# Hybrid decoder layer on one core: the last layer norm's mean taken out of the weights and the residual, its squares on ScalarE

## Chip, core and metric

The kernel runs on one core of a Trainium2 chip. The metric is the device time of one execution in microseconds (us). Engines are called PE (TensorE), DVE (VectorE), ACT (ScalarE), POOL (GpSimd) and SP (SyncE, which here issues every DMA).

## What is computed

One post-norm decoder layer over 256 tokens of width 1024. The input is normalized, projected to 3844 columns, and sent through four mixers (SSD, HGRN2, retention, block attention), each of which gives 256 columns of y. The four are put side by side, multiplied with an output weight, added to the scaled input and normalized again:

```python
def _layernorm(x, g, b):
    xf = x.astype(F32)
    mu = jnp.mean(xf, -1, keepdims=True)
    var = jnp.mean(jnp.square(xf - mu), -1, keepdims=True)
    return ((xf - mu) * lax.rsqrt(var + LN_EPS) * g + b).astype(x.dtype)
...
    y_cat = jnp.concatenate([y_ssd, y_hgrn, y_ret, y_moba], axis=-1).astype(x.dtype)
    y = jnp.einsum('blm,md->bld', y_cat, w_out)
    return _layernorm(DEEPNORM_ALPHA * x + y, ln_g, ln_b)
```

## The kernel before

Everything is in SBUF at once: the 256 tokens are two blocks T = 0, 1 of 128 partitions. Each matmul of float32 data is made of three passes on parts: every operand is split in a high part (rounded, type fp32r) and a low part (the rest), and hi x hi, hi x lo and lo x hi are summed in PSUM. For weights this split is `split_hi` (L215, a copy on ACT, L222) and `split_lo` (L224, a subtraction on DVE, L231). For the mixers' outputs it is `y_split` (L420: ACT at L422, DVE at L423).

The order of the work is written by hand. There are 38 weight tiles of 512 KB: 15 column units of the input projection with two halves each (tiles 0 to 29), then the output weight as four pairs of row blocks (`ORDER`, 256 rows each) with two column halves of 512 each (tiles 30 to 37, shape 128 x 2 x 512, `wr_wo`). The program runs in slots. `begin(slot)` (L1046) issues the load of tile slot + 6 (`load_w`, five raw buffers), splits tile slot + 4 on ACT, runs the mixers' steps that a table `steps` (L1007) lists for this slot, and then makes the low part of tile slot + 4 on DVE. After that come the matmuls of the slot's own tile (`project`). So ACT and DVE take their work in the order in which it is written here, and work of a step stands in the same queue as the weights' splits.

From slot 30 on the matmuls are those of the output projection (`oproj`, L969), in the order of the list at L1064: blocks i = 0, 1, 2 of T = 0 (each 12 matmuls over 512 columns), block 0 of T = 1, block 3 of T = 0, and then the rest of T = 1 by column pieces (512, 256, 256; `OCOLS`). `begin` of slots 30 to 37 stands between them, and four transposes of the retention's y before block 2. The names in the profile are `po` for the sums in PSUM, `whi_wo` and `wlo_wo` for the weight's parts.

The residual (`residual`, L961, one for each T, in slots 21 and 22) makes alpha * x of the first norm's output from rows that a DMA broadcast to all partitions (`load_rows`, tile `rb`). The last norm's rows are loaded into the same buffer right behind, so this second load waits for the second residual. After the last matmul of a column piece `out_add` (L984) adds the residual and takes statistics; after the last piece `out_norm` (L989) joins these, makes the inverse root on POOL (`rsqrt_of`, L251), and applies norm, weight and bias on DVE, with a store per piece.

Of the kernel before, what the change touches and what calls it, by code (L numbers as in the profile page):

```python
# [119 lines left out]
def hybrid_layer(  # L120
# [21 lines left out]
    def sb(shape, name, tag=None, dt=F32, bufs=1):  # L142
        return sp.tile(shape, dt, name=name, tag=tag or name, bufs=bufs)
# [24 lines left out]
    mhalf = cp.tile([P, 8], F32, name="mhalf")  # L168
    nc.gpsimd.memset(mhalf, -0.5)


# [783 lines left out]
    def load_rows(first):  # L955
# [3 lines left out]
        rowt[first] = t  # L959

    def residual(T):  # L961
        rb = rowt[0]
        nc.vector.scalar_tensor_tensor(xn[T], xn[T], ALPHA, rb[:, 0, :], op0=ALU.mult, op1=ALU.mult)
        nc.vector.scalar_tensor_tensor(xn[T], rb[:, 1, :], ALPHA, xn[T], op0=ALU.mult, op1=ALU.add)

# [15 lines left out]

    fst = [sb([P, len(OCOLS[T]) - 1, 6], f"fst{T}") for T in range(NT)]

    def out_add(T, n):  # L984
        cs = slice(OCOLS[T][n], OCOLS[T][n + 1])
        nc.vector.tensor_add(xn[T][:, cs], xn[T][:, cs], po[T, cs.start])  # L986
        nc.vector.bn_stats(fst[T][:, n, :], xn[T][:, cs])

    def out_norm(T):  # L989
        rb = rowt[2]  # L990
        m_ = sb([P, 2], f"fmv{T}")
        nc.vector.bn_aggr(m_, fst[T])
        rs = sb([P, 1], f"frs{T}")
        rsqrt_of(rs, m_[:, 1:2], 1.0, LN_EPS)
        cuts = [slice(a, b) for a, b in zip(OCOLS[T], OCOLS[T][1:])]
        for cs in (slice(0, 512), slice(512, 1024)):
            nc.vector.scalar_tensor_tensor(xn[T][:, cs], xn[T][:, cs], m_[:, 0:1], rb[:, 0, cs],
                                           op0=ALU.subtract, op1=ALU.mult)
        for cs in cuts:
            nc.vector.scalar_tensor_tensor(xn[T][:, cs], xn[T][:, cs], rs[:, 0:1], rb[:, 1, cs],  # L1000
                                           op0=ALU.mult, op1=ALU.add)
            nc.sync.dma_start(out[T * P:(T + 1) * P, cs], xn[T][:, cs])
# [43 lines left out]
    def begin(slot):  # L1046
        if slot < 32:
            load_w(*divmod(slot + 6, 2))
        if slot < 34:
            split_hi(*divmod(slot + 4, 2))  # L1050
        for st in steps.get(slot, []):
            st()
        if slot < 34:
            split_lo(*divmod(slot + 4, 2))

    first_unit()
# [62 lines left out]
```

## Time and profile before

| | before |
|---|---|
| median of 3 runs | 150.22 us (150.21 to 150.48) |
| the profiled execution | 150.22 us, its span 148.5 us |
| PE busy | 136.9 us, 92% of the span |
| DVE busy | 116.4 us, 78% |
| ACT busy | 74.7 us, 50% |
| POOL busy | 17.8 us, 12% |
| mean granted PE clock | 0.977 |

The span runs from the first to the last recorded instruction; the 1.7 us between it and the execution's time lie around it. Busy time is not yet a bound: PE is the engine on the chain that ended last for nearly the whole span, and the others matter where it waits for them.

### The profile page before, as it was taken

Reading aid. Unit: us, or ns where it says so; the run is one execution under the profiler, and the core shown is the slowest. Engines: PE = TensorE matmul, PEld = TensorE weight load, DVE = VectorE, ACT = ScalarE, POOL = GpSimd, SP = SyncE. Lnnn points to the kernel's source line nnn. Section 1 sums busy time; section 2 is a strip of 40 time slices with the busy share of each in tenths; the row PEclk is TensorE's granted clock in tenths of the full one; section 3 lists DMA queues with packets and bytes.
Section 4 is the critical chain, followed back from the end, with each engine's and each line's share of the span. In section 5 each row is a group of like instructions: output and inputs, shape, how many; then the busy total and the mean of one; then the engine's idle time right before and its main releaser. Section 6 shows DMA issues by size and latency. Waiting matters only on the chain.

```text
span 148.5 us, 3256 instructions
## 1 busy us (share of the span) xinstructions
PE 136.9 (92%) x1320; PEld 127.0 (86%) x1320; DVE 116.4 (78%) x240; ACT 74.7 (50%) x120; POOL 17.8 (12%) x23
## 2 busy tenths in 40 slices
PE   5679999999999999999999999999999999999800
PEld 3169999999999998999999999999999988888800
DVE  1789978989495498969897699976889898078681
ACT  3089969643360859699909950053861953000000
POOL 4230000000000000000062018014004000004040
PEclk9968999999999999999999999999999999999995
DMA  4998399989758340647615820279765440000304
GB/s 155 288 385 342 87 321 339 306 302 348 224 151 224 127 109 32 173 182 248 178 75 145 309 118 0 55 238 385 234 228 141 141 141 4 0 0 0 141 0 141
DMA packets 9390, 26.07 MB, mean 176 GB/s; under 512 B 1056, under 2 KB 1696, under 8 KB 9120
## 3 DMA queue, kind: packets, MB, share of 16 engines
q1 hardware_dynamic: 9376, 25.87, 52.9%
q8 instruction: 10, 0.16, 0.5%
q14 instruction: 4, 0.03, 0.1%
HBM read 24.82 MB, written 1.05 MB: 174 GB/s over the span
## 4 chain that ended last, share of the span: by engine, by line
PE 89%; DMA 3%; DVE 3%; SPq 1%; POOLq 1%; POOL 1%; issue 0%; DVEq 0%
PE po L979 5%; PE po L980 5%; PE po L978 5%; PE pj_h_f L343 4%; PE pj_z L406 4%; PE pj_xs L406 4%; PE pj_m_v L406 4%; PE pj_m_k L406 4%; PE pj_h_g L406 4%; PE pj_m_g L406 4%; PE pj_m_q L406 4%; PE pj_bc L406 4%; PE pj_r_k L406 4%; PE pj_r_g L406 4%; PE pj_h_i L406 4%; PE pj_r_v L406 4%
## 5 line engine op out<-in xcount | busy, mean ns | idle before, releaser
L979 PE MATMUL po<-wlo_wo,yhi 128*128 128x512 f32 (+1 forms) x40 | 14.0, 350 | 0.0
L978 PE MATMUL po<-whi_wo,yhi 128*128 128x512 f32 (+1 forms) x40 | 14.0, 349 | 0.0
L980 PE MATMUL po<-whi_wo,ylo 128*128 128x512 f32 (+1 forms) x40 | 13.9, 347 | 0.0
L222 ACT CAST whi_wo<-wr_wo 128x1024 fp32r<-128x1024 f32 x8 | 8.3, 1051 | 3.3 <-DMA wr_wo<-in_wo_dram 1.9
L231 DVE TENSOR_TENSOR wlo_wo<-wr_wo,whi_wo 128x1024 fp32r<-128x1024 f32 x8 | 9.6, 1218 | 0.0
L693 POOL TENSOR_SCALAR_AFFINE_SELECT ra<-ahi 128x1024 fp32r<-128x1024 f32 x1 | 1.1, 1102 | 65.1 <-DVE ahi L689 65.1
L978 PEld LDWEIGHTS po<-whi_wo,yhi 128*128 128x128 f32 x40 | 7.5, 188 | 1.0
L980 PEld LDWEIGHTS po<-whi_wo,ylo 128*128 128x128 f32 x40 | 7.5, 188 | 1.0
L979 PEld LDWEIGHTS po<-wlo_wo,yhi 128*128 128x128 f32 x40 | 7.5, 188 | 1.0
L986 DVE TENSOR_TENSOR xn<-xn,po 128x512 f32<-128x512 f32 (+1 forms) x5 | 2.9, 579 | 5.8 <-PE po L980 5.8
L637 DVE SCALAR_TENSOR_TENSOR cacc_xs<-pj_xs,ch,cacc_xs 128x255 f32<-128x255 f32 (+2 forms) x6 | 2.9, 482 | 4.6 <-ACT cacc_xs L635 4.4
L176 PE MATMUL warm<-warm 128*128 128x512 f32 x6 | 4.6, 939 | 1.5 <-DVE warm L173 1.5
L300 PE MATMUL tr<-ck,xn 128*128 128x128 f32 x16 | 3.9, 378 | 2.3 <-DVE xn L276 2.2
L300 PEld LDWEIGHTS tr<-ck,xn 128*128 128x128 f32 x16 | 2.6, 187 | 3.5 <-DVE xn L276 3.5
L776 ACT ACTIVATE ssq<-sy 128x512 f32<-128x512 f32 x1 | 0.6, 632 | 9.2 <-DVE sy L774 9.2
L263 DVE BATCH_NORM_STATS2 lst<-xt 128x6 f32<-128x512 f32 x4 | 2.8, 694 | 3.1 <-DMA xt<-in_x_dram 3.1
L842 ACT ACTIVATE pe<-pe,mmax 128x128 f32<-128x128 f32 (+1 forms) x8 | 3.5, 445 | 3.0 <-DVE mmax L835 3.0
L176 PEld LDWEIGHTS warm<-warm 128*128 128x128 f32 x6 | 1.7, 311 | 3.6 <-issue 2.1
L406 PE MATMUL pj_z<-whi_z,hhi 128*128 128x260 f32 x16 | 4.6, 289 | 0.0
L222 ACT CAST whi_h_f<-wr_h_f 128x512 fp32r<-128x512 f32 x3 | 1.9, 619 | 5.4 <-DMA wr_h_f<-in_w_dram 5.4
L406 PE MATMUL pj_h_g<-whi_h_g,hhi 128*128 128x256 f32 x16 | 4.6, 287 | 0.0
L406 PE MATMUL pj_m_k<-hhi,whi_m_k 128*128 128x256 f32 x16 | 4.6, 287 | 0.0
(298 smaller groups left out, 547.5 us busy)
## 6 DMA issues: line engine op xcount, KB each, us to landing
wr_wo<-in_wo_dram SPq DMA_DIRECT2D x8, 512.0 KB, 4.8
rb<-in_rows_dram SPq DMA_DIRECT2D x2, 1024.0 KB, 7.8
wr_z<-in_w_dram SPq DMA_DIRECT2D x2, 520.0 KB, 6.8
xt<-in_x_dram SPq DMA_DIRECT2D x4, 256.0 KB, 3.3
wr_h_f<-in_w_dram SPq DMA_DIRECT2D x4, 256.0 KB, 4.6
wr_h_q<-in_w_dram SPq DMA_DIRECT2D x2, 512.0 KB, 5.7
wr_h_i<-in_w_dram SPq DMA_DIRECT2D x2, 512.0 KB, 5.2
wr_m_q<-in_w_dram SPq DMA_DIRECT2D x2, 512.0 KB, 4.8
```

What stands on the lines that cost most here:

```text
L176: nc.tensor.matmul(wb, warm[:, :P], warm, start=True, stop=True)
L222: copy(whi[i, j][:, r, :], t[:, r, :])
L231: nc.vector.tensor_sub(wlo[i, j][:, r, :], t[:, r, :], whi[i, j][:, r, :].bitcast(F32))
L300: nc.tensor.transpose(trb[k][:, T * P:(T + 1) * P], xn[T][:, k * P:(k + 1) * P], ident)
L343: nc.tensor.matmul(ps[n], l[:, n * P:(n + 1) * P], r[:, k, :], start=(k == 0 and q == 0), stop=(k == KT - 1 and q == 2))
L406: nc.tensor.matmul(ps, l, r, start=(n == 0), stop=(n == len(seq) - 1))
L637: nc.vector.scalar_tensor_tensor(a_[:, d:], ps[:, :SEQ - d], tap(3 - d), a_[:, d:], op0=ALU.mult, op1=ALU.add)
L842: nc.scalar.activation(pt[:, h, :], pt[:, h, :], AF.Exp, bias=mmax[:, i:i + 1], accum_out=msum[:, i:i + 1])
L978: nc.tensor.matmul(po[T, c0], yhi[:, k, ts], hi, start=(i == 0 and j == 0), stop=False)
L979: nc.tensor.matmul(po[T, c0], yhi[:, k, ts], lo, start=False, stop=False)
L980: nc.tensor.matmul(po[T, c0], ylo[:, k, ts], hi, start=False, stop=(i == 3 and j == 1))
L986: nc.vector.tensor_add(xn[T][:, cs], xn[T][:, cs], po[T, cs.start])
```

## The change

The layer norm's mean over the 1024 output columns is linear in the sum it is taken of. So the change takes it out of both summands ahead of time. `wo_sum` has ACT go over each raw output weight tile with a copy that also sums a row (in place, two passes of 512 columns). When both column halves of a pair are summed, `wo_split` joins the sums on POOL (an add and a scaling by -1/1024) and then makes the high parts on ACT with this as bias, two passes of 512 per tile, and the low parts on DVE. `residual` sums its second product, scales the sum on DVE, and a pass on ACT adds it as bias. What `out_add` gives then has mean zero; it squares on ACT with a sum over the row, multiplies with the norm's weight on DVE beside it (into `zg`), and adds the sum of squares to the variance. `out_norm` is left with one power on POOL, and one product and add per piece on DVE.

```diff
--- before.py
+++ after.py
@@ -167,6 +167,8 @@
 
     mhalf = cp.tile([P, 8], F32, name="mhalf")
     nc.gpsimd.memset(mhalf, -0.5)
+    epsln = cp.tile([P, 1], F32, name="epsln")
+    nc.gpsimd.memset(epsln, LN_EPS)
 
 
     warm = sb([P, 512], "warm", tag="att")
@@ -958,10 +960,40 @@
         nc.sync.dma_start(t, rows[:, o:o + 2 * DM].to_broadcast([P, 2 * DM]))
         rowt[first] = t
 
+
+
     def residual(T):
         rb = rowt[0]
         nc.vector.scalar_tensor_tensor(xn[T], xn[T], ALPHA, rb[:, 0, :], op0=ALU.mult, op1=ALU.mult)
-        nc.vector.scalar_tensor_tensor(xn[T], rb[:, 1, :], ALPHA, xn[T], op0=ALU.mult, op1=ALU.add)
+        sm_ = sb([P, 1], f"rsum{T}")
+        nc.vector.scalar_tensor_tensor(xn[T], rb[:, 1, :], ALPHA, xn[T], op0=ALU.mult, op1=ALU.add,
+                                       accum_out=sm_)
+        nc.vector.tensor_scalar(sm_, sm_, -1.0 / DM, None, op0=ALU.mult)
+        nc.scalar.activation(xn[T], xn[T], AF.Identity, bias=sm_[:, 0:1])
+
+    wsum = sb([P, 2, 8], "wsum")
+
+    def wo_sum(i, j):
+        for q in range(2):
+            o = 2 * (i - len(UNITS)) + q
+            nc.scalar.activation(raw[i, j][:, q, :], raw[i, j][:, q, :], AF.Copy,
+                                 accum_out=wsum[:, j, o:o + 1])
+
+    def wo_split(i):
+
+        m = 2 * (i - len(UNITS))
+        wm = wsum[:, 0, m:m + 2]
+        nc.gpsimd.tensor_tensor(wm, wm, wsum[:, 1, m:m + 2], op=ALU.add)
+        nc.gpsimd.tensor_scalar(wm, wm, -1.0 / DM, None, op0=ALU.mult)
+        for j in range(2):
+            whi[i, j] = part_tile(i, j, "whi", SPENT_HI)
+            wlo[i, j] = part_tile(i, j, "wlo", SPENT_LO)
+            for q in range(2):
+                nc.scalar.activation(whi[i, j][:, q, :], raw[i, j][:, q, :], AF.Identity,
+                                     bias=wm[:, q:q + 1])
+                nc.vector.scalar_tensor_tensor(wlo[i, j][:, q, :], raw[i, j][:, q, :], wm[:, q:q + 1],
+                                               whi[i, j][:, q, :].bitcast(F32),
+                                               op0=ALU.add, op1=ALU.subtract)
 
 
     po = {}
@@ -979,25 +1011,32 @@
             nc.tensor.matmul(po[T, c0], yhi[:, k, ts], lo, start=False, stop=False)
             nc.tensor.matmul(po[T, c0], ylo[:, k, ts], hi, start=False, stop=(i == 3 and j == 1))
 
-    fst = [sb([P, len(OCOLS[T]) - 1, 6], f"fst{T}") for T in range(NT)]
+    zg = [[sb([P, 512], f"zg{T}{n}", tag=(("sy", "ho"), ("xdt", "xsd"))[T][n]) for n in range(2)]
+          for T in range(NT)]
+    fss = [sb([P, 3], f"fss{T}") for T in range(NT)]
+    fvar = [sb([P, 1], f"fvar{T}") for T in range(NT)]
+
+    def zpart(T, n):
+        c0, c1 = OCOLS[T][n], OCOLS[T][n + 1]
+        return zg[T][c0 // 512][:, c0 % 512:c0 % 512 + c1 - c0]
+
+    def out_var(T, n):
+        nc.vector.scalar_tensor_tensor(fvar[T], fss[T][:, n:n + 1], 1.0 / DM,
+                                       epsln if n == 0 else fvar[T], op0=ALU.mult, op1=ALU.add)
 
     def out_add(T, n):
         cs = slice(OCOLS[T][n], OCOLS[T][n + 1])
         nc.vector.tensor_add(xn[T][:, cs], xn[T][:, cs], po[T, cs.start])
-        nc.vector.bn_stats(fst[T][:, n, :], xn[T][:, cs])
+        nc.scalar.activation(po[T, cs.start], xn[T][:, cs], AF.Square, accum_out=fss[T][:, n:n + 1])
+        nc.vector.tensor_mul(zpart(T, n), xn[T][:, cs], rowt[2][:, 0, cs])
+        out_var(T, n)
 
     def out_norm(T):
-        rb = rowt[2]
-        m_ = sb([P, 2], f"fmv{T}")
-        nc.vector.bn_aggr(m_, fst[T])
         rs = sb([P, 1], f"frs{T}")
-        rsqrt_of(rs, m_[:, 1:2], 1.0, LN_EPS)
-        cuts = [slice(a, b) for a, b in zip(OCOLS[T], OCOLS[T][1:])]
-        for cs in (slice(0, 512), slice(512, 1024)):
-            nc.vector.scalar_tensor_tensor(xn[T][:, cs], xn[T][:, cs], m_[:, 0:1], rb[:, 0, cs],
-                                           op0=ALU.subtract, op1=ALU.mult)
-        for cs in cuts:
-            nc.vector.scalar_tensor_tensor(xn[T][:, cs], xn[T][:, cs], rs[:, 0:1], rb[:, 1, cs],
+        nc.gpsimd.tensor_tensor(rs, fvar[T], mhalf[:, :1], op=ALU.pow)
+        for n, (a, b) in enumerate(zip(OCOLS[T], OCOLS[T][1:])):
+            cs = slice(a, b)
+            nc.vector.scalar_tensor_tensor(xn[T][:, cs], zpart(T, n), rs[:, 0:1], rowt[2][:, 1, cs],
                                            op0=ALU.mult, op1=ALU.add)
             nc.sync.dma_start(out[T * P:(T + 1) * P, cs], xn[T][:, cs])
 
@@ -1046,12 +1085,16 @@
     def begin(slot):
         if slot < 32:
             load_w(*divmod(slot + 6, 2))
-        if slot < 34:
+        if slot < 26:
             split_hi(*divmod(slot + 4, 2))
+        elif slot < 34:
+            wo_sum(*divmod(slot + 4, 2))
         for st in steps.get(slot, []):
             st()
-        if slot < 34:
+        if slot < 26:
             split_lo(*divmod(slot + 4, 2))
+        elif slot < 34 and slot % 2:
+            wo_split((slot + 4) // 2)
 
     first_unit()
     lower_bound()
```

How this moves the instructions, at three places. First ACT, from the first output weight tile on (`yt` is the transposed y, `g_h_g` and `g_m_g` are gates of two mixers). Before:

```order
L222 CAST whi_wo_0_1505<-wr_wo_0_1417 128x1024 [waits DMAHW5_49,PE_49]
L422 CAST yhi<-yt_1507 128x512 [waits PE_49]
L619 ACT_TABLE_LOAD
L619 ACTIVATE g_h_g<-pj_h_g 128x512
L222 CAST whi_wo_1_1573<-wr_wo_1_1473 128x1024 [waits DMAHW6_49]
L222 CAST whi_wo_0_1624<-wr_wo_0_1503 128x1024 [waits DMAHW7_49,PE_49,Activation_49]
L876 ACTIVATE g_m_g<-pj_m_g 128x512 [waits PE_49]
L878 CAST yhi<-mo 128x512 [waits DVE_49]
L222 CAST whi_wo_1_1666<-wr_wo_1_1571 128x1024 [waits DMAHW0_49,Activation_49]
L422 CAST yhi<-yt_1626 128x512 [waits PE_49]
```

With the change:

```order
L979 ACTIVATE wr_wo_0_1432,wsum<-wr_wo_0_1432 128x512 [waits DMAHW5_49]
L979 ACTIVATE wr_wo_0_1432,wsum<-wr_wo_0_1432 128x512
L424 CAST yhi<-yt_1522 128x512 [waits PE_49]
L621 ACT_TABLE_LOAD
L621 ACTIVATE g_h_g<-pj_h_g 128x512
L979 ACTIVATE wr_wo_1_1488,wsum<-wr_wo_1_1488 128x512 [waits DMAHW6_49,Activation_49]
L979 ACTIVATE wr_wo_1_1488,wsum<-wr_wo_1_1488 128x512
L992 ACTIVATE whi_wo_0_1611<-wr_wo_0_1432,wsum 128x512 [waits Activation_49,Pool_49]
L992 ACTIVATE whi_wo_0_1611<-wr_wo_0_1432,wsum 128x512 [waits Activation_49]
L992 ACTIVATE whi_wo_1_1617<-wr_wo_1_1488,wsum 128x512 [waits Activation_49] x2
L979 ACTIVATE wr_wo_0_1518,wsum<-wr_wo_0_1518 128x512 [waits DMAHW7_49,DVE_49]
L979 ACTIVATE wr_wo_0_1518,wsum<-wr_wo_0_1518 128x512
```

The high parts of the first pair now stand behind the sums of both its tiles and wait for POOL, and the next tile and the gate `g_m_g` stand behind them.

Second, DVE at the same place (`rst`, `rmv` and `ro` are the retention's norm, `mo` the attention's gated output). Before:

```order
L612 TENSOR_TENSOR ho<-ho,g_h_g 128x512 [waits DVE_49]
L231 TENSOR_TENSOR wlo_wo_0_1544<-wr_wo_0_1417,whi_wo_0_1505 128x1024 [waits DMAHW5_49]
L939 BN_STATS rst<-reo 128x6 [waits PE_49]
L939 BN_STATS rst<-reo 128x6 x7
L941 BN_AGGR rmv<-rst 128x2 [waits DVE_49] x8
L942 TENSOR_TENSOR ro<-reo,rmv 128x512 [waits DVE_49]
L231 TENSOR_TENSOR wlo_wo_1_1596<-wr_wo_1_1473,whi_wo_1_1573 128x1024 [waits DMAHW6_49,Activation_49]
L877 TENSOR_TENSOR mo<-mbo,g_m_g 128x512 [waits Activation_49]
L879 TENSOR_TENSOR ylo<-mo,yhi 128x512 [waits Activation_49]
```

With the change:

```order
L614 TENSOR_TENSOR ho<-ho,g_h_g 128x512 [waits DVE_49]
L941 BN_STATS rst<-reo 128x6 [waits PE_49]
L941 BN_STATS rst<-reo 128x6 x7
L943 BN_AGGR rmv<-rst 128x2 [waits DVE_49] x8
L944 TENSOR_TENSOR ro<-reo,rmv 128x512 [waits DVE_49]
L994 SCALAR_TENSOR_TENSOR wlo_wo_0_1612<-wr_wo_0_1432,wsum,whi_wo_0_1611 128x512 [waits DMAHW5_49,Activation_49]
L994 SCALAR_TENSOR_TENSOR wlo_wo_0_1612<-wr_wo_0_1432,wsum,whi_wo_0_1611 128x512 [waits Activation_49]
L994 SCALAR_TENSOR_TENSOR wlo_wo_1_1618<-wr_wo_1_1488,wsum,whi_wo_1_1617 128x512 [waits DMAHW6_49,Activation_49]
L994 SCALAR_TENSOR_TENSOR wlo_wo_1_1618<-wr_wo_1_1488,wsum,whi_wo_1_1617 128x512 [waits Activation_49]
L879 TENSOR_TENSOR mo<-mbo,g_m_g 128x512 [waits Activation_49]
L881 TENSOR_TENSOR ylo<-mo,yhi 128x512 [waits Activation_49]
```

The low parts of the first pair went from both sides of the retention's statistics to behind them, and stand together; on POOL the join of the first pair stands behind the two operations for `rrs`:

```order
L254 TENSOR_SCALAR rrs<-rmv 128x8 [waits DVE_49]
L255 TENSOR_TENSOR rrs<-rrs,mhalf 128x8 [waits Pool_49]
L986 TENSOR_TENSOR wsum<-wsum 128x2 [waits Activation_49]
L987 TENSOR_SCALAR wsum<-wsum 128x2 [waits Pool_49]
L986 TENSOR_TENSOR wsum<-wsum 128x2 [waits Activation_49]
L987 TENSOR_SCALAR wsum<-wsum 128x2 [waits Pool_49]
```

Third, DVE after the last matmul (`xn` holds the sum, `frs` the inverse root). Before:

```order
L986 TENSOR_TENSOR xn_111<-xn_111,po_768_1778 128x256 [waits PE_49]
L987 BN_STATS fst_217<-xn_111 128x6 [waits DVE_49]
L992 BN_AGGR fmv_1872<-fst_217 128x2 [waits DVE_49]
L997 SCALAR_TENSOR_TENSOR xn_111<-xn_111,fmv_1872,rb_1346 128x512 [waits DVE_49]
L997 SCALAR_TENSOR_TENSOR xn_111<-xn_111,fmv_1872,rb_1346 128x512
L1000 SCALAR_TENSOR_TENSOR xn_111<-xn_111,frs_1874,rb_1346 128x512 [waits DVE_49,Pool_49]
```

With the change:

```order
L1029 TENSOR_TENSOR xn_113<-xn_113,po_768_1833 128x256 [waits PE_49]
L1031 TENSOR_TENSOR zg_222<-xn_113,rb_1361 128x256 [waits DVE_49]
L1024 SCALAR_TENSOR_TENSOR fvar_226<-fss_224,fvar_226 128x1 [waits Activation_49]
L1039 SCALAR_TENSOR_TENSOR xn_113<-zg_221,frs_1932,rb_1361 128x512 [waits Pool_49]
```

Aggregation and the two subtractions of the mean are gone, a product of 256 columns and a 128x1 operation stand in their place, and between these ACT squares the piece.

## Rows read from the trace of the kernel before

**Rows 1.** Page, part 4: share of the chain that ended last, by engine.

```profile
PE 89%; DMA 3%; DVE 3%; SPq 1%; POOLq 1%; POOL 1%; issue 0%; DVEq 0%
```

**Rows 2.** Timeline of PE, output projection: start us, length us, engine, line, operation.

```profile
117.73 0.39 PE L978 MATMUL po<-whi_wo,yhi 128*128 128x512 f32 x1
...
120.48 0.39 PE L978 MATMUL po<-whi_wo,yhi 128*128 128x512 f32 x1
...
123.61 0.47 PE L978 MATMUL po<-whi_wo,yhi 128*128 128x512 f32 x1
...
129.28 0.40 PE L978 MATMUL po<-whi_wo,yhi 128*128 128x512 f32 x1
...
140.34 0.28 PE L980 MATMUL po<-whi_wo,ylo 128*128 128x256 f32 x1
```

**Rows 3.** Groups by line, low parts: busy us, mean ns of one, idle before.

```profile
L231 DVE TENSOR_TENSOR wlo_wo<-wr_wo,whi_wo 128x1024 fp32r<-128x1024 f32 x8 | 9.6, 1218 | 0.0
```

**Rows 4.** Timeline of ACT at the first output weight tiles.

```profile
104.57 1.05 ACT L222 CAST whi_wo<-wr_wo 128x1024 fp32r<-128x1024 f32 x1 [0.35 <-DMA wr_wo<-in_wo_dram]
...
106.12 1.28 ACT L619 ACT_TABLE_LOAD   x1
107.41 0.60 ACT L619 ACTIVATE g_h_g<-pj_h_g 128x512 f32<-128x512 f32 x1
107.91 1.04 ACT L222 CAST whi_wo<-wr_wo 128x1024 fp32r<-128x1024 f32 x1
```

**Rows 5.** Timeline of ACT, 256-column passes: plain ones; with bias and sum.

```profile
14.19 0.41 ACT L313 CAST hhi<-hf 128x256 fp32r<-128x256 f32 x1
14.50 2.00 ACT L222 CAST whi_h_q<-wr_h_q 128x1024 fp32r<-128x1024 f32 x2
...
62.89 0.49 ACT L842 ACTIVATE pe<-pe,mmax 128x256 f32<-128x256 f32 x1
...
63.39 0.50 ACT L842 ACTIVATE pe<-pe,mmax 128x256 f32<-128x256 f32 x1
```

**Rows 6.** Timelines of POOL and DVE: an early power; the retention's norm.

```profile
6.50 0.57 POOL L268 TENSOR_TENSOR lrs<-lrs,mhalf 128x1 f32<-128x1 f32 x1
...
108.05 0.69 DVE L610 TENSOR_TENSOR g_h_g<-g_h_g,rw 128x512 f32<-128x512 f32 x1 [0.94 <-ACT g_h_g L619]
...
112.18 0.63 DVE L941 BATCH_NORM_AGGREGATE rmv<-rst 128x2 f32<-128x6 f32 x8
...
112.89 0.20 POOL L252 TENSOR_SCALAR rrs<-rmv 128x8 f32<-128x8 f32 x1 [11.04 <-DVE rmv L941]
113.17 1.64 POOL L253 TENSOR_TENSOR rrs<-rrs,mhalf 128x8 f32<-128x8 f32 x1
```

**Rows 7.** Timelines of DVE and SP: a sum read out; residual and row load.

```profile
62.95 0.08 DVE L831 DVE_READ_ACCUMULATOR2_ANT mmax<- 128x1 f32 x1
63.06 0.17 DVE L835 TENSOR_SCALAR mmax<-mmax 128x2 f32<-128x2 f32 x1
...
93.64 1.22 DVE L964 SCALAR_TENSOR_TENSOR xn<-rb,xn 128x1024 f32<-128x1024 f32 x1
...
94.90 0.33 SPq L958 DMA_DIRECT2D rb<-in_rows_dram  x1
```

**Rows 8.** Timeline of the tail, after the last matmul.

```profile
140.66 0.42 DVE L986 TENSOR_TENSOR xn<-xn,po 128x256 f32<-128x256 f32 x1 [1.24 <-PE po L980]
...
141.90 0.75 POOL L252 TENSOR_SCALAR frs<-fmv 128x1 f32<-128x1 f32 x1 [6.13 <-DVE fmv L992]
142.73 0.95 POOL L253 TENSOR_TENSOR frs<-frs,mhalf 128x1 f32<-128x1 f32 x1
143.71 1.54 DVE L1000 SCALAR_TENSOR_TENSOR xn<-xn,frs,rb 128x512 f32<-128x512 f32 x3 [0.45 <-POOL frs L253]
```

**Rows 9.** Early pause of PE (timeline); window after it: busy times, then PEclk.

```profile
8.38 2.54 PE L300 MATMUL tr<-ck,xn 128*128 128x128 f32 x10 [2.23 <-DVE xn L276]
...
8.21:11.62 3.41, 3.22 (x15) 2.82 (x16) 2.86 (x8) 2.88 (x6) 0.81 (x2) 0.55 1.04 394
```

## The prediction, made before the change was run

> **What bounds the kernel now.** I read the chain of waits first, then the timeline of TensorE, then those of ScalarE, VectorE and POOL around the output weights, and last the tail after the last matmul. The chain [rows 1] gives PE 89% of the span, so nothing that another engine does costs time until PE waits for it, and anything that makes PE wait costs its full length. At the end the timeline [rows 2] shows PE without a gap: the output projection starts at 117.73, its second block (block 1 of the first 128 rows) at 120.48, its third at 123.61 (behind four transposes), the fifth at 129.28, and the last matmul ends at 140.34 + 0.28 = 140.62. From there to the end of the span is 7.9 us in which PE is done and only the last layer norm and the stores run. The change shortens this tail and pays for it in the stretch in front of it, so both have to be priced. The profiled execution took 150.22 us, which is also the median of the runs; the sum below is made against it.
>
> **The tail, a gain.** Today, after the last add of 256 columns starts at 140.66, the way to the first output product at 143.71 is 3.05 us: add 0.42, statistics and their aggregation, then two operations on POOL of 0.75 and 0.95 [rows 8]. In the change it is: add 0.42, a hand-over of about 0.1, a square of 256 columns on ScalarE that also sums (a plain pass of 256 is 0.41 long, the sum adds some 0.1 [rows 5]), one VectorE operation on 128x1 of about 0.17 (as the small one in [rows 7]) and a single power on POOL. That power takes 0.95 today with VectorE working beside it; with little beside it, it took 0.57 [rows 6]. In the change VectorE waits for it, so I take 0.6. The sum with hand-overs is 0.42 + 0.1 + 0.5 + 0.17 + 0.1 + 0.6 = 1.9, against 3.05: **a gain of 1.15**; with 0.95 for the power it is 0.8. The product with the norm's weight moves beside the square and costs nothing as long as the square is the longer. What follows 143.71 is unchanged: three products, and their stores.
>
> **The residual, early.** Each of the two residuals gets a sum on its second product, a 128x1 scaling on VectorE and a pass over 1024 columns on ScalarE. Reading out a sum takes 0.08 and a small operation 0.17 [rows 7], so about 0.25 each on VectorE. ScalarE's two passes of some 1.1 fall where it mostly waits (before 98). But the load of the last norm's rows is issued when the second product of the second residual ends (93.64 + 1.22 = 94.86, issue at 94.90), and the loads of the output weights stand behind it on the same queue [rows 7]: they come about 0.25 later. Up to 2 us that this delays PE before 120 would be swallowed by the wait below.
>
> **The output weights, the price.** Each of the eight raw tiles is today one ScalarE pass of 1024 columns, 1.04 [rows 4], and one VectorE subtraction, 1.22 [rows 3]. The change makes of it two summing passes of 512, then, when both column halves of a pair of row blocks are summed and POOL has joined them, two passes of 512 with a bias. A 512 pass holds ScalarE for 0.50, from its start at 107.41 to the next at 107.91 [rows 4]. A 256 pass with sum and bias has 0.50 from start to start (62.89 to 63.39), a plain one 0.31 (14.19 to 14.50) [rows 5], so sum and bias cost 0.19 together. A summing pass is then 0.60 and a biased one 0.59: **2.38 per tile instead of about 1**. Between bounds: without any extra 2.0, with the extra of 0.19 on every pass 2.76. I take 2.38, as rows 5 have both extras once.
>
> Walked through in ScalarE's new order:
> - Tile 30 lands 0.25 later than the 104.57 of [rows 4], 104.8; its sums end at 106.0. A split of the transposed y (0.5), the table load that today starts at 106.12 and ends at 107.41, and the gate (0.5) end at 108.4; sums of tile 31 at 109.6.
> - ScalarE then waits for the join. On POOL it stands behind the two operations for the retention norm. Today these start when VectorE has its statistics, at 112.18 + 0.63 = 112.81, which is 5.40 after the gate's start at 107.41; one subtraction of 1.14 has moved out of that way, so 4.26 after 107.9: 112.2. POOL then needs 2.00 (to 113.17 + 1.64) [rows 6], 114.2. The join is two small operations: 0.20 each as at 112.89 [rows 6], or 0.75 each as at 141.90 beside VectorE work [rows 8]. VectorE waits for ScalarE at these points, so I take 0.20, which is 0.45 with the hand-over, or 0.65 from the end of a sum: 114.65.
> - High parts of the first pair end at 117.0. PE needs them from 117.73: **no wait here**.
> - Sums of tile 32 to 118.2, gate 118.7, then VectorE's product (0.1 + 0.69) and its split (0.5), 120.05; sums of tile 33 to 121.25; join at 121.9 (a split lies beside it); high parts to 124.25. VectorE's last low part is ready about 0.8 later. PE wants this pair at 120.48 and gets its last half at 125.05.
> - Sums of tile 34 to 125.45, gate 125.95, sums of 35 to 127.15, join 127.8, high parts to 130.15; last low part 130.95, and two matmuls on it to 131.5. Today this block ends at about 126.4: 12 matmuls after 123.61. **PE is 5.1 late.**
> - Sums of 36 and 37, a split, and the high parts end at 135.55, the last low part with its matmuls at 136.9. PE, which has two blocks of 2.8 of its own to do after 131.5, gets there at 137.1: nothing more is added.
>
> So the last matmul ends near 145.7, and the time is 150.22 + 5.1 - 1.15 = **154.2 us**. Without any extra per pass, 12 halves x 0.19 come off, of which about 1.8 are not hidden behind the first join; joins at 0.45 take off 0.4 more: 152.0. With every join at 1.75 from the end of its sum (both operations at 0.75) three joins add 3.3: 157.5.
>
> **Rivals.**
> 1. The weights' work stays hidden, and only the tail is left: 150.22 - 1.15 = **149.1**, faster. For it: ScalarE is half idle over the whole span, and PE's order and its loads are unchanged. Against it: the second pair's high parts would have to be out by 120.5 and the third's by 123.6, 4 to 6 us before my walk has them, and most of the walk is plain passes at measured prices. It decides at the second output block.
> 2. The waits cost PE its clock. In the first 10 us PE stood still for 2.23 us, and the granted clock fell: over 8.21 to 11.62 its mean is 0.55, close to the lower level of 1.2 GHz [rows 9]. The waits that I forecast before 132 are of 1 to 2 us with thin work between them. One such stretch at half clock is 3.4 us long and loses 1.7 us of dense matmuls: **155.9**, slower. It decides only if the stretch falls on dense work, after 131.
> 3. The summing residual product runs at half rate. The second products then take 1.22 more each, 2.4 together; the row load waits for the second of them and the output weights for the row load, so ScalarE's whole walk starts 2.4 later: **156.6**. Against it: the plain form takes 1.22 for 1024 columns [rows 7], as the two-input subtraction does [rows 3], so nothing is halved there now. The Trainium skill's page "Vector Engine (DVE) Microarchitecture Reference", in "Points that are easy to get wrong", says that this form with two SBUF sources that are not bf16 has half the throughput, since both read ports are taken and none is left to read the accumulator back. No row here shows the form with a sum on such sources.
>
> **Chances.** My forecast 0.67 (with slow joins as its upper part), the clock 0.17, the half rate 0.06, hidden work 0.07; the rest is hidden work in part. A measurement here can tell about 0.2% (0.3 us) from no change. Faster: 0.07, the first rival. Within 0.2%: 0.02, if about a fifth of my wait is left. Slower: 0.91. The range takes in the bounds of my case, 152.0 to 157.5, and with them the second and third rivals; it leaves out the first and the tails.
>
> **What the changed profile would show.** If I am right: ScalarE almost without a gap from about 115 to 135 (the splits, sums and high parts); PE idle before the first-half matmuls of the second and third output blocks, released by ScalarE's high parts, 5 us in sum; little wait at the fifth block; a join of under 0.5 us on POOL; and after the last matmul 1.9 us to the first output product. I am wrong if PE shows no gap between 117 and 135 (rival 1), if the granted clock there is below 1 (rival 2), if the summing residual row is near 2.4 (rival 3), or if the summing passes are far from 0.6 from start to start.

## The result, and the profile after

| | before | after |
|---|---|---|
| median | 150.22 us (150.21 to 150.48) | 155.96 us (155.65 to 156.25) |
| the profiled execution | 150.22 us, span 148.5 us | 155.65 us, span 153.9 us |
| PE busy | 136.9 us, 92% | 139.8 us, 91% |
| DVE busy | 116.4 us, 78% | 116.6 us, 76% |
| ACT busy | 74.7 us, 50% | 92.1 us, 60% |
| POOL busy | 17.8 us, 12% | 17.2 us, 11% |

The ratio is 1.0374, interval 1.0332 to 1.0416: slower, inside the range of the prediction and 1.8 us above its number. The same kernel was measured twice more, beside the later experiments: 154.65 us and 154.92 us (ratios 1.0270 and 1.0330). Its 16 executions in the three measurements lie at 154.1 to 154.7 and at 155.4 to 156.6; profiles of both kinds are read below. The ratios leave out runs counted as slow, among them the two of the second measurement at 156.6, which its median takes in.

First the chain of waits (the page's part 4) and the costliest groups (part 5) of the changed kernel; a group's columns are busy us, mean ns of one, and the idle time of the engine before it.

```profile
PE 51%; DVE 12%; ACT 11%; DMA 11%; issue 8%; POOL 2%; SPq 1%; POOLq 0%; DVEq 0%
...
L1010 PE MATMUL po<-whi_wo,yhi 128*128 128x512 f32 (+1 forms) x40 | 14.6, 365 | 2.7 <-ACT whi_wo L992 2.7
...
L994 DVE SCALAR_TENSOR_TENSOR wlo_wo<-wr_wo,wsum,whi_wo 128x512 fp32r<-128x512 f32 x16 | 11.0, 746 | 4.8 <-ACT whi_wo L992 4.8
L992 ACT ACTIVATE whi_wo<-wr_wo,wsum 128x512 fp32r<-128x512 f32 x16 | 10.3, 712 | 5.9 <-POOL wsum L987 5.6
...
L979 ACT ACTIVATE wr_wo<-wr_wo 128x512 f32<-128x512 f32 x16 | 9.9, 618 | 0.3 <-DMA wr_wo<-in_wo_dram 0.3
```

PE's share of the chain went from 89% [rows 1] to 51%. In its place stands what leads to the output weights: DVE's work up to the second residual, the load of the first output weight tile, ACT's sums, the retention norm on DVE and POOL, ACT's high parts. The shares are only a hint, since the chain follows POOL's `issue` for 7.15 us from 141.43 to 148.58, where PE is at work until 147.35. Read from below, the groups tell the order: ACT waits for POOL's `wsum` (5.6), DVE for ACT's high parts (4.8), PE for the same high parts (2.7).

ACT's timeline shows the walk of the prediction, from the first sum to the four pairs of high parts.

```profile
103.92 0.63 ACT L979 ACTIVATE wr_wo<-wr_wo 128x512 f32<-128x512 f32 x1 [0.27 <-DMA wr_wo<-in_wo_dram]
...
107.53 0.62 ACT L979 ACTIVATE wr_wo<-wr_wo 128x512 f32<-128x512 f32 x1
108.05 0.19 ACT L979 ACTIVATION_READ_ACCUMULATOR wr_wo<-wr_wo 128x1 f32 x1
108.14 0.62 ACT L979 ACTIVATE wr_wo<-wr_wo 128x512 f32<-128x512 f32 x1
...
113.82 2.57 ACT L992 ACTIVATE whi_wo<-wr_wo,wsum 128x512 fp32r<-128x512 f32 x4 [4.96 <-POOL wsum L987]
...
121.33 2.57 ACT L992 ACTIVATE whi_wo<-wr_wo,wsum 128x512 fp32r<-128x512 f32 x4
...
127.43 2.56 ACT L992 ACTIVATE whi_wo<-wr_wo,wsum 128x512 fp32r<-128x512 f32 x4 [0.61 <-POOL wsum L987]
...
133.06 2.57 ACT L992 ACTIVATE whi_wo<-wr_wo,wsum 128x512 fp32r<-128x512 f32 x4
```

A summing pass takes 0.61 from start to start (107.53 to 108.14; [rows 4] have 0.50 for a plain one). The first pair's high parts begin 4.96 after ACT had nothing left to do. POOL's timeline shows why:

```profile
111.38 0.20 POOL L254 TENSOR_SCALAR rrs<-rmv 128x8 f32<-128x8 f32 x1 [9.47 <-DVE rmv L943]
111.66 1.64 POOL L255 TENSOR_TENSOR rrs<-rrs,mhalf 128x8 f32<-128x8 f32 x1
113.26 0.20 POOL L986 TENSOR_TENSOR wsum<-wsum 128x2 f32<-128x2 f32 x1
113.55 0.24 POOL L987 TENSOR_SCALAR wsum<-wsum 128x2 f32<-128x2 f32 x1
```

The sums were there before 109; the join runs at 113.26, since the retention norm's two operations stand ahead of it and wait for DVE until 111.38. The join itself is short.

PE's timeline of the output projection shows what of it reaches the end.

```profile
117.64 0.39 PE L1010 MATMUL po<-whi_wo,yhi 128*128 128x512 f32 x1
...
122.10 0.49 PE L1010 MATMUL po<-whi_wo,yhi 128*128 128x512 f32 x1 [1.54 <-ACT whi_wo L992]
122.89 0.50 PE L1011 MATMUL po<-wlo_wo,yhi 128*128 128x512 f32 x1 [0.29 <-DVE wlo_wo L994]
...
126.38 0.66 PE L419 MATMUL yt<-ck,ro 128*128 128x128 f32 x4 [0.68 <-DVE ro L952]
128.21 0.50 PE L1010 MATMUL po<-whi_wo,yhi 128*128 128x512 f32 x1 [1.17 <-ACT whi_wo L992]
128.99 0.68 PE L1011 MATMUL po<-wlo_wo,yhi 128*128 128x512 f32 x1 [0.29 <-DVE wlo_wo L994]
129.47 0.63 PE L1012 MATMUL po<-whi_wo,ylo 128*128 128x512 f32 x1
129.90 0.63 PE L1010 MATMUL po<-whi_wo,yhi 128*128 128x512 f32 x1
...
147.07 0.28 PE L1012 MATMUL po<-whi_wo,ylo 128*128 128x256 f32 x1
```

The first block starts as before (117.64; 117.73 in [rows 2]). The third starts at 128.21 and not at 123.61, 4.60 later; the pause before its first low part adds 0.55 (128.21 to 128.99, where neighbours usually start 0.23 apart). That is a delay of 5.2; the profile counts 4.0 of it as idle time (1.54, 0.29, 0.68, 1.17 and 0.29 in the rows above). But the last matmul is 6.73 later than before: 1.5 more. They are in the rows after 128.99, where matmuls start 0.43 apart (129.47 to 129.90), not 0.23. The windows of the same execution give the clock (columns: length, busy us of PE, PEld, DVE, ACT, POOL with their instructions, granted PE clock, DMA share, GB/s):

```profile
117.00:128.00 11.00, 7.52 (x35) 5.23 (x34) 6.43 (x10) 9.49 (x24) 0.82 (x4) 1.00 0.48 143
128.00:132.50 4.50, 4.00 (x10) 2.94 (x11) 2.74 (x4) 4.50 (x13) 0.00 (x0) 0.63 0.03 5
132.50:136.00 3.50, 3.50 (x22) 3.11 (x21) 2.87 (x5) 2.98 (x5) 0.41 (x2) 0.99 0.00 0
```

From 128.00 to 132.50 the mean granted clock is 0.63, most of that stretch near the lower level of 1.2 GHz, and that is the dense work behind the third block's wait.

Last the tail, on DVE:

```profile
147.38 0.42 DVE L1029 TENSOR_TENSOR xn<-xn,po 128x256 f32<-128x256 f32 x1 [0.96 <-PE po L1012]
147.84 0.42 DVE L1031 TENSOR_TENSOR zg<-xn,rb 128x256 f32<-128x256 f32 x1
148.38 0.16 DVE L1024 SCALAR_TENSOR_TENSOR fvar<-fss,fvar 128x1 f32<-128x1 f32 x1
149.21 1.54 DVE L1039 SCALAR_TENSOR_TENSOR xn<-zg,frs,rb 128x512 f32<-128x512 f32 x3 [0.67 <-POOL frs L1036]
```

From the last add to the first output product it is 1.83, where [rows 8] have 3.05.

### The profile page after: what moved, and what is told of

The parts are those of the page before. It is cut to its first block, busy times and chain, and to the rows that moved or that the text cites. A ratio compares the mean times of both kernels' runs of the same rounds, so it can differ in the third digit from the quotient of the medians.

```text
span 153.9 us, 3331 instructions
## 1 busy us (share of the span) xinstructions
PE 139.8 (91%) x1320; PEld 127.0 (83%) x1320; DVE 116.6 (76%) x251; ACT 92.1 (60%) x172; POOL 17.2 (11%) x30
## 4 chain that ended last, share of the span: by engine, by line
PE 51%; DVE 12%; ACT 11%; DMA 11%; issue 8%; POOL 2%; SPq 1%; POOLq 0%; DVEq 0%
DMA wr_wo<-in_wo_dram 5%; PE pj_h_f L345 4%; ACT wr_wo L979 4%; PE pj_z L408 4%; PE pj_xs L408 4%; PE pj_m_v L408 4%; PE pj_m_k L408 4%; PE pj_bc L408 4%; PE pj_m_q L408 4%; PE pj_h_i L408 4%; PE pj_h_q L408 4%; PE pj_r_q L408 4%; ACT whi_wo L992 3%; DMA wr_h_f<-in_w_dram 3%; DMA ret<-in_ret_dram 2%
## 5 line engine op out<-in xcount | busy, mean ns | idle before, releaser
L1011 PE MATMUL po<-wlo_wo,yhi 128*128 128x512 f32 (+1 forms) x40 | 14.8, 370 | 0.6 <-DVE wlo_wo L994 0.6
L1012 PE MATMUL po<-whi_wo,ylo 128*128 128x512 f32 (+1 forms) x40 | 14.6, 365 | 0.0
L994 DVE SCALAR_TENSOR_TENSOR wlo_wo<-wr_wo,wsum,whi_wo 128x512 fp32r<-128x512 f32 x16 | 11.0, 746 | 4.8 <-ACT whi_wo L992 4.8
L992 ACT ACTIVATE whi_wo<-wr_wo,wsum 128x512 fp32r<-128x512 f32 x16 | 10.3, 712 | 5.9 <-POOL wsum L987 5.6
L979 ACT ACTIVATE wr_wo<-wr_wo 128x512 f32<-128x512 f32 x16 | 9.9, 618 | 0.3 <-DMA wr_wo<-in_wo_dram 0.3
L1030 ACT ACTIVATE po<-xn 128x512 f32<-128x512 f32 (+1 forms) x5 | 2.6, 517 | 9.5 <-DVE xn L1029 9.5
L972 ACT ACTIVATE xn<-xn,rsum 128x1024 f32<-128x1024 f32 x2 | 2.3, 1156 | 8.1 <-DVE rsum L971 8.1
L178 PE MATMUL warm<-warm 128*128 128x512 f32 x6 | 5.2, 1038 | 1.5 <-DVE warm L175 1.5
L408 PE MATMUL pj_m_g<-hhi,whi_m_g 128*128 128x256 f32 x16 | 4.6, 288 | 0.0
L408 PE MATMUL pj_r_k<-hhi,whi_r_k 128*128 128x256 f32 x16 | 4.6, 287 | 0.0
```

The lines of the kernel that those rows point to most:

```text
L178: nc.tensor.matmul(wb, warm[:, :P], warm, start=True, stop=True)
L408: nc.tensor.matmul(ps, l, r, start=(n == 0), stop=(n == len(seq) - 1))
L979: nc.scalar.activation(raw[i, j][:, q, :], raw[i, j][:, q, :], AF.Copy, accum_out=wsum[:, j, o:o + 1])
L992: nc.scalar.activation(whi[i, j][:, q, :], raw[i, j][:, q, :], AF.Identity, bias=wm[:, q:q + 1])
L994: nc.vector.scalar_tensor_tensor(wlo[i, j][:, q, :], raw[i, j][:, q, :], wm[:, q:q + 1], whi[i, j][:, q, :].bitcast(F32), op0=ALU.add, op1 ...
L1011: nc.tensor.matmul(po[T, c0], yhi[:, k, ts], lo, start=False, stop=False)
```

## The experiments

Four numbers of each profile carry all of them: the start of ACT's first pass on the output weights, of PE's first output block, of the last matmul, and the rest of the span from there. The start of the first block scatters with what happens in the first 20 us, whatever the kernel (from 20 to 117 PE has no gap in any of them). Where PE does not wait, it is 22.6 from there to the last matmul in every profile. Where PE waits for ACT, the end follows ACT's first pass instead: the kernel with the extra matmuls has 28.74 and 27.99 from the first block, but 41.65 and 41.61 from ACT's first pass.

| profile of | ACT first pass | first block | last matmul | first block to last matmul | rest of the span |
|---|---|---|---|---|---|
| before | 104.57 | 117.73 | 140.34 | 22.61 | 8.16 |
| after | 103.92 | 117.64 | 147.07 | 29.43 | 6.83 |
| after, second measurement | 104.90 | 118.64 | 148.04 | 29.40 | 6.86 |
| after, third measurement | 104.11 | 117.76 | 145.73 | 27.97 | 6.87 |
| old tail, new weights | 104.76 | 118.20 | 147.87 | 29.67 | 8.13 |
| new tail, old weights | 104.20 | 117.42 | 140.04 | 22.62 | 6.86 |
| join ahead | 104.26 | 117.65 | 142.37 | 24.72 | 6.83 |
| 14 extra matmuls | 104.79 | 117.70 | 146.44 | 28.74 | 6.86 |
| the same, second time | 104.83 | 118.45 | 146.44 | 27.99 | 6.86 |
| sums with the high parts | 104.18 | 117.95 | 140.57 | 22.62 | 6.83 |
| the same, join late | 104.19 | 117.53 | 141.47 | 23.94 | 6.83 |

**The new tail alone.** The output weights are split as before; residual and tail are the change's.

```diff
-        if slot < 26:
+        if slot < 34:
             split_hi(*divmod(slot + 4, 2))
-        elif slot < 34:
-            wo_sum(*divmod(slot + 4, 2))
```

(and the like for `split_lo` and `wo_split`)

> The changed kernel with the output weights split as before, uncentred (the mean is then only taken out of the residual, not out of the product with the weights). Theory A (the loss is all in ScalarE's work on the weights, the tail is a gain of 1.2): no gap on PE between 117 and 135, 149.0 us, between 148.7 and 149.4. Rival B (the new tail or the residual passes cost too, and part of the 5.7 us is theirs): 150.2 or more.

Measured 149.06 us, ratio 0.9907 (0.9878 to 0.9936). PE has no wait between 117 and the last matmul, first block to last matmul is 22.62 (22.61 before), and the rest of the span is 1.30 shorter. The slowdown is all in the work on the weights, and the tail is a gain.

**The tail without the residual's mean either.** As above, and `residual` is that of before.

```diff
-        nc.vector.scalar_tensor_tensor(xn[T], rb[:, 1, :], ALPHA, xn[T], op0=ALU.mult, op1=ALU.add,
-                                       accum_out=sm_)
-        nc.vector.tensor_scalar(sm_, sm_, -1.0 / DM, None, op0=ALU.mult)
-        nc.scalar.activation(xn[T], xn[T], AF.Identity, bias=sm_[:, 0:1])
+        nc.vector.scalar_tensor_tensor(xn[T], rb[:, 1, :], ALPHA, xn[T], op0=ALU.mult, op1=ALU.add)
```

> Only the new tail: the weights split as before and the residual without its sum, its scaling and its ScalarE pass, so no mean is taken out at all. Theory A (the residual's part is free): as the run with the new tail and the centred residual, ratio to before 0.990 (0.987 to 0.993). Rival B (the sums and the two passes of 1024 cost time in front of the output weights): 0.5 us or more below that, ratio under 0.987.

Measured 149.49 us, 0.9938 (0.9917 to 0.9958); first block to last matmul 22.62, rest 6.85. The ratio is a little above the expected range and far from rival B's. Leaving the sums, the scaling and the two ACT passes of the residual out gains nothing, so their cost is hidden.

**The weights alone.** Centred weights and residual, but the norm at the end as before.

```diff
-        nc.scalar.activation(po[T, cs.start], xn[T][:, cs], AF.Square, accum_out=fss[T][:, n:n + 1])
-        nc.vector.tensor_mul(zpart(T, n), xn[T][:, cs], rowt[2][:, 0, cs])
-        out_var(T, n)
+        nc.vector.bn_stats(fst[T][:, n, :], xn[T][:, cs])
```

(and `out_norm` as in the kernel before)

> The changed kernel with the tail of the kernel before (statistics, aggregation, two POOL operations, subtraction of the mean); weights and residual stay centred. Theory A (tail and weights add up): 1.2 us above the changed kernel, 157.1 (156.7 to 157.6). Rival B (the new tail only gains while PE ends early): within 0.5 us of the changed kernel.

Measured 157.33 us, 1.0466 (1.0439 to 1.0494). The rest of the span is back at 8.13, so the new tail's 1.3 is seen from this side too, on top of the waits. The median is 1.4 above the first measurement of the change, but 2.7 above the one taken beside it (154.65): all executions here (156.78 to 158.05) lie some 1.3 above the change's upper group, and the profile has a granted clock of 0.70 from 128 to 132.5 (0.63 in the change's first profile). Why none lies 1.3 above the lower group is open.

**The join ahead of the slot's steps.** POOL's two operations are issued right behind the second tile's sums, and so ahead of the retention norm's.

```diff
+            if slot % 2:
+                wo_join((slot + 4) // 2)
         for st in steps.get(slot, []):
```

> The changed kernel with one thing moved: POOL's join of a pair's sums is issued ahead of the slot's steps, so ahead of the retention norm's two POOL operations; every pass stays. Theory A1 (ScalarE's wait of 4.96 us for the first join starts the delay, and the doubled passes only fill what is left): high parts of the first pair start near 109.4 instead of 113.8, PE waits about 1.5 us in all, at the third block, the granted clock stays at 1, time 150.4 (149.8 to 151.2). Rival A2 (the passes alone are too many, the join's place does not matter): 154 or more.

Measured 151.39 us, 1.0065 (1.0041 to 1.0088): most of the loss is gone, though the time is 0.2 above the expected range. ACT and PE in this kernel:

```profile
110.16 2.56 ACT L996 ACTIVATE whi_wo<-wr_wo,wsum 128x512 fp32r<-128x512 f32 x4 [0.96 <-POOL wsum L986]
...
124.23 2.57 ACT L996 ACTIVATE whi_wo<-wr_wo,wsum 128x512 fp32r<-128x512 f32 x4 [0.61 <-POOL wsum L986]
```

```profile
125.01 0.49 PE L1014 MATMUL po<-whi_wo,yhi 128*128 128x512 f32 x1 [1.17 <-ACT whi_wo L996]
125.79 0.51 PE L1015 MATMUL po<-wlo_wo,yhi 128*128 128x512 f32 x1 [0.29 <-DVE wlo_wo L998]
...
142.37 0.28 PE L1016 MATMUL po<-whi_wo,ylo 128*128 128x256 f32 x1
```

ACT waits 0.96 for the first join, not 4.96, and the first and third pair's high parts are 3.7 and 3.2 earlier. The second block's wait is gone, the third's stays, and first block to last matmul is 2.11 longer than before. Against the tail's 1.3 that leaves about 0.8; 0.65% of 150.2 us is 1.0. In the change's third profile (read below), whose third block keeps its clock, first block to last matmul is 5.36 longer than before; moving the join alone takes 3.25 of this off. The fall of the clock went with it (granted clock 1.00 in this profile from 117 to 147).

**PE kept at work in the waits.** 14 matmuls of 512 columns that nobody reads, 6 ahead of the second block, 3 and 5 around the start of the third.

> The changed kernel with 14 extra matmuls of 512 columns on PE whose results nobody reads, put where it waits (6 before the second block, 3 before the transposes, 5 behind them; 3.2 us of work). Theory A (the clock that falls after the waits costs 1.7 us at the third block): granted clock 1.00 from 117 to 147, time 154.3 (153.8 to 154.8). Rival B (the third block is held by ScalarE and VectorE anyway, and the slow clock costs nothing): 155.6 to 156.3.

Measured 154.77 us, 1.0308 (1.0267 to 1.0349), at the upper edge of theory A's range. Its third block:

```profile
129.86 0.50 PE L1011 MATMUL po<-wlo_wo,yhi 128*128 128x512 f32 x1 [0.29 <-DVE wlo_wo L994]
...
146.44 0.28 PE L1012 MATMUL po<-whi_wo,ylo 128*128 128x256 f32 x1
```

From the third block's first low part to the last matmul it is 16.58, against 18.08 in the changed kernel (128.99 to 147.07), and from 128 to 132.5 the granted clock is 1.00. So the extra matmuls kept the clock, and that is worth 1.50 there. The median however is only 1.2 below that of the change, which was not measured beside it, and two executions, 155.69 and 156.23, are as long as the change's, so both were measured again, side by side:

> The changed kernel itself, beside the three below on one chip. Both theories: 155.6 to 156.3 us, ratio to before 1.033 to 1.042.

> The kernel with the 14 unread matmuls a second time, now beside the changed kernel on one chip. Theory A (the fallen clock costs time at the third block): 1.0 to 1.7 us below the changed kernel in these runs, granted clock 1.00 from 117 to 147. Rival B (the clock costs nothing, since ScalarE and VectorE hold the block): within 0.4 us of it.

Measured 154.65 us (1.0270, 1.0247 to 1.0293) for the change and 154.70 us (1.0288, 1.0263 to 1.0312) with the extra matmuls: no difference in the medians, so the expected gap is a miss, and the change itself came out 1.0 below its expected range. But the change's executions lie apart here, four at 154.09 to 154.73 and two at 156.62 and 156.63, while those with the extra matmuls lie at 154.19 to 155.20. The profile of the change is one of the long ones, and its third block is at the lower clock again, with matmuls 0.42 apart:

```profile
129.96 0.62 PE L1011 MATMUL po<-wlo_wo,yhi 128*128 128x512 f32 x1 [0.29 <-DVE wlo_wo L994]
130.38 0.63 PE L1012 MATMUL po<-whi_wo,ylo 128*128 128x512 f32 x1
...
148.04 0.28 PE L1012 MATMUL po<-whi_wo,ylo 128*128 128x256 f32 x1
```

From the first low part to the last matmul it is 18.08, as in the change's first profile, with a granted clock of 0.74 from 128 to 132.5; the second profile with the extra matmuls has 16.54. So the change by itself may not lose its clock there every time. A third measurement was to tell:

> The changed kernel a third time. Theory A (the fall of the clock at the third block costs 1.5 us and comes in some executions only): single executions lie in two groups, 154.0 to 155.2 without it and 155.6 to 156.7 with it, and a profiled one with the fall takes 18.1 us from the first low-part matmul of the third block to the start of the last matmul, one without it 16.6. Rival B (the earlier calls differed by the chip alone): one group.

Measured 154.92 us (1.0330, 1.0279 to 1.0381), executions from 154.27 to 156.41; the profiled one took 154.34. Its windows and its third block:

```profile
117.00:128.00 11.00, 9.00 (x36) 6.59 (x35) 6.61 (x10) 9.49 (x25) 0.81 (x4) 0.84 0.49 143
128.00:132.50 4.50, 3.83 (x15) 2.89 (x16) 2.74 (x4) 4.50 (x12) 0.00 (x0) 1.00 0.02 5
```

```profile
127.04 0.84 PE L419 MATMUL yt<-ck,ro 128*128 128x128 f32 x4
128.38 0.50 PE L1010 MATMUL po<-whi_wo,yhi 128*128 128x512 f32 x1 [0.50 <-ACT whi_wo L992]
129.17 0.50 PE L1011 MATMUL po<-wlo_wo,yhi 128*128 128x512 f32 x1 [0.29 <-DVE wlo_wo L994]
...
145.73 0.28 PE L1012 MATMUL po<-whi_wo,ylo 128*128 128x256 f32 x1
```

Here the clock fell too, but earlier, between 117 and 128 (mean 0.84), on the second block. PE would have waited there anyway: the wait for the third block's weights is 0.50, not 1.17, and the transposes are not waited for at all. From the first low part to the end it is 16.56, as with the extra matmuls. Counted from ACT's first pass to the last matmul, the three profiles without a fall on the third block agree: 41.62 here, 41.65 and 41.61 with the extra matmuls. So do the three with it: 43.15 and 43.14 in the change's first two profiles, 43.11 with the old tail. So the fall costs 1.5 where it hits the third block and next to nothing where it hits the second. That the executions without a profile part into two groups for the same reason is not shown. It fits the groups' distance, but 155.39 and 155.58 lie just under the edge expected for the upper group, and the two long executions with the extra matmuls (155.69 and 156.23) have no profile. Both groups came up on one chip, so the chip is not the reason; what decides which block the fall hits, no run here explains.

**Sums taken in the pass that makes the high parts.** The bias is not needed in the high part: `whi` is made of the raw weights as before, the pass that makes it sums as it goes, and DVE puts the mean into the low part, (raw + mean) - high. One ACT pass per half, not two; the join is ahead of the steps.

```diff
     def wo_sum(i, j):
+        whi[i, j] = part_tile(i, j, "whi", SPENT_HI)
...
-            nc.scalar.activation(raw[i, j][:, q, :], raw[i, j][:, q, :], AF.Copy,
+            nc.scalar.activation(whi[i, j][:, q, :], raw[i, j][:, q, :], AF.Copy,
                                  accum_out=wsum[:, j, o:o + 1])
...
-                nc.scalar.activation(whi[i, j][:, q, :], raw[i, j][:, q, :], AF.Identity,
-                                     bias=wm[:, q:q + 1])
...
+            if slot % 2:
+                wo_join((slot + 4) // 2)
```

> The high part is made of the uncentred weight in two passes that also sum the row, so the eight tiles have no pass of their own for the sum; the mean goes into the low part alone on VectorE, behind POOL's join, which is issued ahead of the slot's steps. ScalarE then has 1.2 us per tile instead of 2.4, and no wait for POOL. Theory A: PE waits under 0.5 us, 149.2 us (148.8 to 149.8), below both kernels. Rival (VectorE's low parts, four passes of 0.67 per pair behind the join, come too late for PE): 150.5 or more, with PE waiting for VectorE.

Measured 149.35 us, 0.9937 (0.9910 to 0.9964), and again:

> The version with the sum taken in the pass that makes the high part, again, beside the changed kernel. Theory A: ratio to before 0.994 (0.991 to 0.997), no wait of PE from 117 on.

Measured 149.09 us, 0.9920 (0.9878 to 0.9962). Both intervals lie below 1: this version is 0.6 to 0.8% faster than the kernel before, and beats the change too. The windows of its first profile:

```profile
117.00:128.00 11.00, 11.00 (x56) 9.18 (x55) 9.66 (x15) 6.87 (x21) 2.03 (x6) 1.00 0.29 90
128.00:132.50 4.50, 4.50 (x27) 3.91 (x26) 2.25 (x4) 0.70 (x2) 0.00 (x0) 1.00 0.00 0
```

PE is busy without a gap, 22.62 from first block to last matmul as before, and the gain of the tail is left.

**The same with the join late.** One line moved: the join back behind the slot's steps, where the change has it.

> The same version with POOL's join back where the change has it, behind the slot's steps. Theory A (only VectorE's low parts wait for the join now; ScalarE does not): low parts of the first pair start 2 us later, near 114.5, the attention's product and with it ScalarE's next splits slip by as much, and PE waits 0.5 to 1 us at the second block: 0.4 to 1.0 us above the version with the early join. Rival B (the slack swallows it): within 0.3 us of it.

Measured 150.52 us, 0.9996 (0.9968 to 1.0024). That is 1.4 above the version with the early join measured beside it, more than the 0.4 to 1.0 expected. The high parts no longer wait for the join, but the low parts do, on DVE, and PE waits for them:

```profile
114.09 2.74 DVE L996 SCALAR_TENSOR_TENSOR wlo_wo<-wr_wo,wsum,whi_wo 128x512 fp32r<-128x512 f32 x4 [1.81 <-POOL wsum L987]
```

```profile
121.23 0.50 PE L1013 MATMUL po<-wlo_wo,yhi 128*128 128x512 f32 x1 [0.55 <-DVE wlo_wo L996]
...
124.96 0.51 PE L1013 MATMUL po<-wlo_wo,yhi 128*128 128x512 f32 x1 [0.25 <-DVE wlo_wo L996]
```

First block to last matmul is 1.33 longer than before, which gives the tail's gain back. So both halves of the repair are needed. They do not add up, and neither can be called the larger cause: of the change's 5.36, moving the join alone leaves 2.11, the cheaper passes alone leave 1.33, both together nothing. And the cheaper passes are two things at once, one ACT pass less and high parts that do not wait for the join; no run parts these.

## Why the prediction was right, and where it fell short

The forecast was a gain in the tail, a larger loss at the second and third output blocks, and 154.2 us in all. Step by step:

- **Tail, 1.9 against 3.05.** Right: 1.83. The square starts 0.45 after the add, POOL's power took 0.56 (0.6 was taken, not the 0.95 of [rows 8]; at the 0.57 of [rows 6] DVE was not idle either, it ran statistics from 6.67 to 7.36), and the product with the norm's weight is hidden beside the square. Over the whole rest of the span the gain is 1.3, a little over the 1.15.
- **Residual, hidden.** Right, by the run without it. The row load is issued at 94.75, no later than the 94.90 of [rows 7], and 1.26 after the start of the second product in both kernels; so the 0.25 by which the weights were to come later was nothing. ACT's first pass came at 103.92 in this profile and at 104.11 to 104.95 in the others with the residual's sums, where 104.8 was forecast.
- **Half rate for the summing product (rival 3).** Refuted:

```profile
93.49 1.23 DVE L969 SCALAR_TENSOR_TENSOR xn<-rb,xn 128x1024 f32<-128x1024 f32 x1
94.64 0.08 DVE L969 DVE_READ_ACCUMULATOR xn<-rb,xn 128x1 f32 x1
```

  In these rows of DVE's timeline of the changed kernel the form with a sum takes 1.23, the plain one 1.22 [rows 7], and the sum is read out in 0.08. The rule of the Trainium skill's page "Vector Engine (DVE) Microarchitecture Reference" ("Points that are easy to get wrong") would have made this row about 2.4, as the prediction worked it out; the row does not agree.
- **Passes at 0.60 and 0.59.** Nearly right: 0.61 from start to start for a sum, and 0.62 for a biased one (four in 2.57, of which the last is 0.71 long). **Joins at 0.45.** Nearly right: 0.53 for the first (0.20 and 0.24 with a gap of 0.09) and 0.49 for the second (120.80 to 121.29).
- **The first join behind the retention norm, high parts at 114.65.** Right, and the step that matters most. Counted from ACT's first pass, the four pairs began after 9.90, 17.41, 23.51 and 29.14 in the profile; the forecast had 9.85, 17.1 and 23.0 for the first three. No wait at the first block, waits at the second and third, none at the fifth, all as forecast.
- **PE 5.1 late.** The term that was mis-sized, by 1.0 without the clock. From ACT's first pass to the last matmul the forecast has 40.6 (104.8 to 145.7, less 0.28 for the last matmul's length); the execution at 154.34 has 41.62. Half of this 1.0 comes from the passes and the gaps between the pairs. The other half is at the third block: I let PE end its block 0.55 behind the last low part. In fact it starts 0.77 after ACT has begun the pair (127.61 to 128.38), stands again before the first low part, and then has ten more matmuls of its own to do; the pair's begin to the block's end is 4.24 (to 131.85), not 3.7. In that execution the walk began 0.7 earlier than forecast, so 154.34 came close to 154.2 partly by luck.
- **The clock (rival 2).** I gave the fall a chance of 0.17 and 155.9, which is my sum and 1.7 more for one stretch at the lower clock. The first measurement, 155.65 to 156.25, is this rival's and not my sum's: its profile has the fall on the third block, at a cost of 1.5. That my range held 155.96 was in part luck: its upper part was worked out from slow joins, and the joins were fast. The rival's condition, that the fall costs time only on dense work, held as well, but that work began at 129 and not after 131. Two of the change's three profiles have the fall there, so 0.17 looks too low; how often it comes is not known.
- **Rival 1, hidden work.** Refuted for the change as it is: the new tail alone gives its 149.1, and so do the sums taken with the high parts (149.35 and 149.09), but with the change's own passes and join PE waits.

The signs that the prediction named came out: ACT nearly without a gap from 114 to 135, a delay of 5.2 at two blocks, joins of about 0.5, 1.8 in the tail. Of the idle time at the two blocks, 2.7 was released by ACT's high parts as forecast; 0.6 waited for low parts and 0.68 for the retention's output (L952) ahead of the transposes. The sign of rival 2, a clock below 1 in the same stretch, came out as well, and by it the sum alone was too low.

## What to carry to other kernels

An engine that is half idle over the span can still be the bound of a stretch: walk its queue through that stretch, with every wait in it, before new work is put there. A two-operation join costs what stands ahead of it in its queue, not only its own 0.5 us; issue it as soon as its inputs are there. And where a correction can ride on a pass that exists (here the low part's), the pass that was to carry it need not be added.

## What the runs showed of the hardware that I had not expected

- **A small POOL operation can last as long as DVE's.** The join's add on 128x2 took 0.20 in most places and 1.00 in one, beside DVE work, in all three profiles that sum with the high parts. Two rows of the first of them, from POOL's timeline:

```profile
117.50 0.19 POOL L986 TENSOR_TENSOR wsum<-wsum 128x2 f32<-128x2 f32 x1 [3.93 <-ACT whi_wo L980]
...
120.91 1.00 POOL L986 TENSOR_TENSOR wsum<-wsum 128x2 f32<-128x2 f32 x1 [2.91 <-ACT whi_wo L980]
```

  In the second place DVE had two-input work from 118.53 to 121.87 (four low parts, then L952 from 121.18 for 0.69), and POOL's add ended at 121.91 with it. It is argued from the times, not tried apart, that the two engines share something there.
- **A sum costs ACT 0.09 of a pass and not the 0.19 that its read-out row shows**: the pass after it starts 0.09 behind that row's start (108.05 to 108.14).
- **Behind waits of 0.7 to 1.8 us with thin work between them the PE clock fell**, from the full 2.4 GHz to the lower level, in all three profiles of the change and in the one with the old tail, on the third block or on the second. With the waits partly filled by matmuls it did not fall there (granted clock 1.00 from 117 to 147 in both profiles with the extra matmuls), nor with the one wait of the kernel with the join ahead (1.17 and 0.29).
